# Four small moves in a fused MoBA and retention block: x reloaded from ScalarE's queue, more products at the first columns, two chunks put ahead of MoBA, the last broadcasts in other banks

## The chip, the cores and the metric

The kernel runs on one core of a Trainium2 chip. The core has five engines that run side by side: PE (TensorE, matrix products, with its weight loads shown apart as PEld), DVE (VectorE), ACT (ScalarE), POOL (GpSimd) and SP (SyncE, which here only starts transfers). PE writes its results to PSUM, which has eight banks of 128 x 512 floats. Everything else is kept in SBUF. The metric is the device time of one execution in microseconds (us). PE's clock stands at one of two levels, 1.2 or 2.4 GHz, and the profile gives what was granted as a share of the higher one.

## What is computed

One decoder block on 512 tokens of width 1024, all in float32. The core of the reference:

```
ada = silu(c) @ w_ada + b_ada            # 6 vectors: sh1, sc1, g1, sh2, sc2, g2
h = rms_norm(x, ln1_w) * (1 + sc1) + sh1
mq, mk, mv, rq, rk, rv, rg, ga, gr = split(h @ w_in)
a_out = moba_attention(rope(mq), rope(mk), mv)       # 8 heads of 64, blocks of 256
r_out = head_group_norm(retention(rope(rq), rope(rk), rv))   # 8 heads, values of 128
merged = sigmoid(ga) * (a_out @ w_moba_o) + sigmoid(gr) * ((silu(rg) * r_out) @ w_ret_o)
x = x + g1 * (merged @ w_out)
h2 = rms_norm(x, ln2_w) * (1 + sc2) + sh2
x = x + g2 * (square(relu(h2 @ w_ff1)) @ w_ff2)      # inner width 4096
return rms_norm(x, final_norm_w)
```

MoBA lets a query see its own block of 256 keys causally, and the chosen fully past blocks. With 512 tokens there are two blocks, so the choice is only whether the first is seen by the second. Retention is causal attention with a decay per head in place of the softmax, and each head's output is normalised by its own mean and variance.

## The kernel before

**Products.** Each float32 operand is split into a high part and a remainder (`hi`, `lo`). A product is three matmuls (`mm3`, lines 220 to 223): high by high, and the two mixed ones. For a weight tile of 128 x 1024, ACT makes `whi` (line 188) and POOL makes `wlo` in four pieces of 256 columns (line 182). The raw weights land in a ring of three buffers (`load_raw`, line 175), and the split ones have four buffers each. A raw buffer is free again when POOL has read it.

**First columns (lines 324 to 343).** The six adaLN vectors come from sums over `w_ada`. ACT and DVE add the products of each column block into `adaacc`, and PE turns the sums to columns (`ada_columns`, line 283). DVE forms the shift and scale `mod` (lines 288, 289), ACT applies them to the transposed x in bank PT and writes the high part `hh` (lines 302, 303), and DVE writes the remainder `hl` (line 306). PE's first real products (lines 373, 376) wait for `hh`. Until then the function `busy(n)` (line 133) issues n matmuls of ones by ones into a bank that nobody reads. `busy(3)` stands behind the first column sums.

**MoBA and the chunks.** While attention runs, PE also does the projections that are still owed. They stand in `queue` as generators, one for each 256 output columns. One step of such a generator is a chunk of two k-tiles, six matmuls. `fill(n)` issues the next n chunks. The first queue holds 11 generators of 8 chunks: 88. Ahead of MoBA `fill(9)` issues nine. Then come the scores of the first head in four tiles (`moba_scores`, lines 596, 597), with two chunks behind each, and one more chunk. In each of the 8 heads there are four turns. A turn transposes the probabilities into the one PT bank (`moba_turn`, line 627). ACT and DVE split them (`th`, `tl`, lines 227, 230), and PE multiplies the turn before with the values (`moba_values`, lines 635, 636). Two chunks may be issued after each turn and one more at each head's start. That is 9 + 8 + 1 + 72 = 90 places for 88 chunks. PE's order is written out by hand; the orders of ACT, DVE and POOL in this stretch are set by the scheduler. The rotations of later projections (`rope`: copies on ACT in line 511, DVE lines 515 to 523; `qs` in lines 534, 535; `kh`, `kl` in lines 551 to 556) stand in a list `later`, a few of whose steps are taken at each turn. The softmax of a tile is DVE lines 602 to 611, ACT's Exp in line 612 and ACT's scaling copy in line 614.

**Retention's norm.** `ret_norm(h)` (line 784) broadcasts a row of factors over the partitions by one matmul into bank PT, and DVE reads it (`zf`, line 786). For heads 4 to 7 it is called one after the other with two chunks behind each, while the owed gates `gr` are projected.

**Output projection and second norm.** `merge` forms `merged` k-tile by k-tile (DVE lines 1029 to 1033, ACT's `mh` in line 1032). PE multiplies it with `w_out`, the first half of the columns into `wo0`, then the second half with weights `woh`, `wol` (ACT line 227 and POOL line 230 of `load_late`). `x2` is x loaded again, 512 KB for each of four token tiles, issued on SP (line 1082). Its buffers lie where tiles of the merge lay. `residual` (lines 1096, 1097) multiplies a product by g1 and adds it to `x2`. `square` (lines 1108, 1109) takes the sum of squares and its root on ACT; the root needs another table in ACT than the one before. `scale2` (lines 1113, 1114) scales on DVE, `turn2` transposes on PE (line 1124), DVE and ACT apply the second shift and scale (lines 1131, 1129), and DVE splits to `h2h` and `h2l` (lines 229, 230 again). Then the MLP's first products start (`ff1_part`). Here the orders of PE, DVE and ACT are written by hand: the products of token tile t, its residual, its square, and behind the products of tile 2 the transposes of tile 0.

## Time and profile before

| | |
|---|---|
| time, median of 3 runs | 882.7 us (882.34 to 882.77) |
| the profiled execution's own time | 883.12 us |
| its span, first to last instruction | 881.3 us |
| mean granted clock | 0.991 |
| busy: PE / DVE / ACT / POOL | 847.6 / 458.6 / 407.1 / 500.1 us |
| moved by DMA | 108.41 MB, mean 123 GB/s |

The time of an execution has 1.8 us around the span. Times in the rows are counted from the span's start. In the list of instructions a row shows when it starts, how long it takes, the engine, the line and operation, what is written from what, and in brackets how long the engine had been idle before it and what ended that wait. A row with x2 merges two neighbours. PE's matmuls overlap: one of 512 columns shows 0.39 us, but the next starts 0.227 us later.

### The profile page before, as it was taken

The numbers are of one execution on the slowest core, as the hardware profiler recorded it, in microseconds if no ns is written. First come the engines' busy times: TensorE is split into PE (matmuls) and PEld (weight loads), VectorE is DVE, ScalarE is ACT, GpSimd is POOL, SyncE is SP. The second block draws the span as 40 slices with busy tenths as digits, with TensorE's granted clock in tenths as the row PEclk, the third lists the DMA queues.
The fourth block names the chain that finished last, engine by engine and source line by source line (L and its number), as shares of the span: only waits on it lengthen the run. The fifth ranks groups of instructions, "written<-read, shape, count | busy, mean of one in ns | idle before, by whom it ended". The sixth has DMA issues, their size and how long they took to land. (4 is left out here: it accounts for less than half of the span.)

```text
span 881.3 us, 11801 instructions
## 1 busy us (share of the span) xinstructions
PE 847.6 (96%) x4138; PEld 708.8 (80%) x4138; DVE 458.6 (52%) x897; ACT 407.1 (46%) x697; POOL 500.1 (57%) x622
## 2 busy tenths in 40 slices
PE   7899999999999999999999899999999999999996
PEld 4777877898788898788887689888888888888885
DVE  5877677677878879853466584203304022222224
ACT  4558988897645547654223243223332211222124
POOL 3465445346545456565546366977777755555564
PEclk9999999999999999999999989999999999999998
DMA  9964222313363443413453633533433232322302
GB/s 278 305 201 132 72 72 72 97 48 97 102 198 120 130 146 111 153 48 96 157 178 119 239 106 97 180 96 121 142 96 96 96 99 97 100 103 98 100 25 96
DMA packets 104426, 108.41 MB, mean 123 GB/s; under 512 B 4832, under 2 KB 93360, under 8 KB 104368
## 3 DMA queue, kind: packets, MB, share of 16 engines
q1 hardware_dynamic: 104224, 107.47, 39.4%
q8 instruction: 32, 0.52, 0.3%
q14 instruction: 26, 0.21, 0.1%
q10 hardware_dynamic: 144, 0.20, 0.1%
HBM read 105.55 MB, written 2.10 MB: 122 GB/s over the span
## 5 line engine op out<-in xcount | busy, mean ns | idle before, releaser
L182 POOL TENSOR_TENSOR wlo<-raw,whi 128x256 fp32r<-128x256 f32 x524 | 409.1, 813 | 284.6 <-ACT whi L188 243.1
L188 ACT ACTIVATE whi<-raw 128x1024 fp32r<-128x1024 f32 x126 | 132.7, 1058 | 189.8 <-PE ps_O L223 104.9
L221 PE MATMUL ps_acc<-hh,whi 128*128 128x512 f32 x304 | 119.8, 394 | 0.0
L222 PE MATMUL ps_acc<-hl,whi 128*128 128x512 f32 x304 | 118.7, 391 | 0.0
L223 PE MATMUL ps_acc<-hh,wlo 128*128 128x512 f32 x304 | 118.7, 390 | 0.0
L221 PE MATMUL ps_acc<-h2h,whi 128*128 128x512 f32 (+1 forms) x288 | 106.2, 369 | 1.1 <-DVE h2h L229 1.1
L222 PE MATMUL ps_acc<-h2l,whi 128*128 128x512 f32 (+1 forms) x288 | 106.2, 369 | 0.3 <-DVE h2l L230 0.3
L223 PE MATMUL ps_acc<-h2h,wlo 128*128 128x512 f32 (+1 forms) x288 | 106.0, 368 | 0.0
L229 DVE CAST fh<-act 128x512 fp32r<-128x512 f32 x32 | 16.2, 515 | 132.5 <-PE ps_O L222 132.5
L223 PEld LDWEIGHTS ps_acc<-hh,wlo 128*128 128x128 f32 x304 | 57.1, 188 | 12.4
L221 PEld LDWEIGHTS ps_acc<-hh,whi 128*128 128x128 f32 x304 | 57.2, 188 | 10.2
L222 PEld LDWEIGHTS ps_acc<-hl,whi 128*128 128x128 f32 x304 | 57.2, 188 | 10.1
L221 PEld LDWEIGHTS ps_acc<-h2h,whi 128*128 128x128 f32 x288 | 54.9, 190 | 10.1 <-DVE h2h L229 1.6
L222 PEld LDWEIGHTS ps_acc<-h2l,whi 128*128 128x128 f32 x288 | 54.9, 191 | 9.3 <-DVE h2l L230 0.7
L223 PEld LDWEIGHTS ps_acc<-h2h,wlo 128*128 128x128 f32 x288 | 55.0, 191 | 8.8
L222 PE MATMUL ps_acc<-wlo,fh 128*128 128x512 f32 (+1 forms) x136 | 52.1, 383 | 0.0
L223 PE MATMUL ps_acc<-whi,fl 128*128 128x512 f32 (+1 forms) x136 | 52.1, 383 | 0.0
L221 PE MATMUL ps_acc<-whi,fh 128*128 128x512 f32 (+1 forms) x136 | 52.1, 383 | 0.0
L847 DVE SCALAR_TENSOR_TENSOR ada_acc<-ada_raw,cact,ada_acc 128x256 f32<-128x256 f32 x48 | 31.2, 649 | 31.9 <-DMA ada_raw<-in_w_ada_dram 31.0
L1201 ACT ACTIVATE relu<-ps_acc 128x512 f32<-128x512 f32 x32 | 18.8, 588 | 62.4 <-PE ps_acc L223 62.4
L823 DVE TENSOR_TENSOR g<-g,ps_acc 128x256 f32<-128x256 f32 x4 | 1.7, 421 | 80.1 <-PE ps_acc L822 80.1
L1202 POOL TENSOR_TENSOR act<-relu 128x512 f32<-128x512 f32 x32 | 34.5, 1078 | 14.1 <-ACT relu L1201 14.0
(291 smaller groups left out, 1861.3 us busy)
## 6 DMA issues: line engine op xcount, KB each, us to landing
raw<-in_w_ff_dram SPq DMA_DIRECT2D x64, 512.0 KB, 3.5
raw<-in_w_in_dram SPq DMA_DIRECT2D x32, 512.0 KB, 3.7
ada_raw<-in_w_ada_dram SPq DMA_DIRECT2D x64, 256.0 KB, 3.1
raw<-in_w_in_dram SPq DMA_DIRECT2D x36, 256.0 KB, 3.5
wada<-in_w_ada_dram SPq DMA_DIRECT2D x32, 256.0 KB, 5.2
x<-in_x_dram SPq DMA_DIRECT2D x8, 512.0 KB, 6.0
raw<-in_w_ret_o_dram SPq DMA_DIRECT2D x8, 512.0 KB, 3.6
dec<-in_k_decay_dram SPq DMA_DIRECT2D x8, 256.0 KB, 4.6
```

Of the source, the lines that this page charges most:

```text
L182: eng.tensor_sub(lo[:, cs], src[:, cs], hi[:, cs].bitcast(F32))
L188: ACT.activation(hi, raw, AF.Copy)
L221: PE.matmul(o, lh, rh, start=first, stop=False)
L222: PE.matmul(o, lh, rl, start=False, stop=False)
L223: PE.matmul(o, ll, rh, start=False, stop=last)
L229: eh.tensor_copy(hi, src)
L823: DVE.tensor_add(dst[:, n0 : n0 + 256], dst[:, n0 : n0 + 256], cp[:, 0:256])
L847: eng.scalar_tensor_tensor(acc, raw[:, 0, :], cact[:, 2 * k2 : 2 * k2 + 1], acc, op0=ALU.mult, op1=ALU.add)
L1201: ACT.activation(r, a, AF.Relu)
L1202: POOL.tensor_mul(act[n], r, r)
```

## The change

Five edits, four of them moves:

- `busy(3)` behind the first column sums becomes `busy(7)`: four more matmuls of ones.
- `fill(9)` ahead of MoBA becomes `fill(11)`: two chunks move from the end of the queue's run to its start.
- `ret_norm` of heads 4 to 7 takes a bank of tag S (three banks) in place of PT (one).
- The four loads of `x2` go from SP's queue to ACT's, and are to stand behind ACT's last `mh` copy.
- A root of one column, whose result nobody reads, is put on ACT behind the same copy, so that ACT's table for roots is loaded there.

```
@@ first columns
     cp = ada_columns(a)
-    busy(3)
+    busy(7)
     mod = modulation(0, cp)
@@ ret_norm
-        rp = ps("PT")
+        rp = ps("PT" if h < 4 else "S")
@@ ahead of MoBA
-    fill(9)
+    fill(11)
     for t in (3, 2, 1, 0):
         moba_scores(0, t)
         fill(2)
@@ reload of x
     for t in range(NT):
         x2.append(B.tile([P, D], F32, name=f"x2_{t}"))
-        dma(x2[t], xs[t * P : (t + 1) * P, :])
+        with tc.issue_after(merged[-1]):
+            ACT.dma_start(x2[t], xs[t * P : (t + 1) * P, :])
@@ behind the definition of residual
+    root = W2.tile([P, P], F32, name="root")[:, :1]
+    with tc.issue_after(merged[-1]):
+        ACT.activation(root, epsc, AF.Sqrt)
     for t in range(NT):
         residual(W2, t, 0, wo0[t], g1)
```

ACT at the end of the merge, before. `mh` is the last of the merge, `woh` are weights of the second half, `y,rs` is the square of a token tile, `whi` a weight tile of the MLP:

```order
L1032 ACTIVATE mh_4636<-m_5110 128x512
L227 ACTIVATE woh_5281<-raw 128x512
L227 ACTIVATE woh_5287<-raw 128x512
L1108 ACTIVATE y_5308,rs_5309<-x_0_5235 128x1024
L1109 ACT_TABLE_LOAD
L1109 ACTIVATE rs_5309<-rs_5309,epsc 128x1
L188 ACTIVATE whi<-raw 128x1024 x2
```

The same place now:

```order
L1032 ACTIVATE mh_4640<-m_5114 128x512
L1084 DMA x_0_5239<-in_x_dram 128x1024
L1084 DMA x_1_5241<-in_x_dram 128x1024
L1084 DMA x_2_5243<-in_x_dram 128x1024
L1084 DMA x_3_5245<-in_x_dram 128x1024
L227 ACTIVATE woh_5287<-raw 128x512
L227 ACTIVATE woh_5293<-raw 128x512
L1104 ACT_TABLE_LOAD
L1104 ACTIVATE root<-epsc 128x1
L1114 ACTIVATE y_5314,rs_5315<-x_0_5239 128x1024
L1115 ACTIVATE rs_5315<-rs_5315,epsc 128x1
L188 ACTIVATE whi<-raw 128x1024 x2
```

Four loads stand ahead of the last two `woh` copies, the fourth of them with a wait for the transfer of the first of these two copies' raw weights, and the table load has left the place between the square and its root. On SP the four loads of x are gone from between the MLP's first raw tile and the loads of g2 and the final norm's weights.

ACT behind the `kh` copies of the first MoBA head, before, up to just ahead of the scaling copy of the last of the head's four tiles (128x128):

```order
L605 ACTIVATE pr,stat<-ps_S 128x256
L612 ACT_TABLE_LOAD
L612 ACTIVATE pr,stat<-ps_S,stat 128x512
L706 ACTIVATE gate_904<-ps_acc 128x512
L612 ACTIVATE pr,stat<-ps_S,stat 128x384
L614 ACTIVATE pr<-pr,stat 128x512
L614 ACTIVATE pr<-pr,stat 128x384
L612 ACTIVATE pr,stat<-ps_S,stat 128x256
L188 ACTIVATE whi<-raw 128x1024
L614 ACTIVATE pr<-pr,stat 128x256
L612 ACTIVATE pr,stat<-ps_S,stat 128x128
L706 ACTIVATE gate_960<-ps_acc 128x512
```

The same place now, up to the scaling of the third tile:

```order
L534 ACTIVATE qs<-roped 64x512
L511 ACTIVATE sw<-ps_acc 32x512 x2
L605 ACTIVATE pr,stat<-ps_S 128x256
L612 ACT_TABLE_LOAD
L612 ACTIVATE pr,stat<-ps_S,stat 128x512
L188 ACTIVATE whi<-raw 128x1024
L614 ACTIVATE pr<-pr,stat 128x512
L612 ACTIVATE pr,stat<-ps_S,stat 128x384
L612 ACTIVATE pr,stat<-ps_S,stat 128x256
L614 ACTIVATE pr<-pr,stat 128x384
L614 ACTIVATE pr<-pr,stat 128x256
```

Between the `kh` copies and the scaling copy of the last tile there now stand three copies of line 511, both copies of line 534 and one weight copy of line 188 more than before; the rest is the same work in another order.

PE at the last MoBA head, now. In the order before, the two turns stood with two chunks (twelve matmuls) between them:

```order
L627 MATMUL ps_PT<-ident,pr 128x128 x2
L635 MATMUL ps_O<-th,vm_724 128x384
L636 MATMUL ps_O<-tl,vm_724 128x384
L627 MATMUL ps_PT<-ident,pr 128x128
L635 MATMUL ps_O<-th,vm_751 128x256
L636 MATMUL ps_O<-tl,vm_751 128x256
L635 MATMUL ps_O<-th,vm_754 128x128
L636 MATMUL ps_O<-tl,vm_754 128x128
```

Nothing stands between the third turn's transposes (x2) and those of the fourth but the products of the turn before. From the first retention scores on PE's order is as before.

## Rows read from the trace of the kernel before

**Rows 1.** Page part 1, then stages: length, busy per engine, PEclk, DMA share, GB/s

```profile
PE 847.6 (96%) x4138; PEld 708.8 (80%) x4138; DVE 458.6 (52%) x897; ACT 407.1 (46%) x697; POOL 500.1 (57%) x622
...
95.00:225.00 130.00, 125.81 (x704) 106.95 (x703) 93.97 (x263) 109.61 (x237) 63.51 (x78) 1.00 0.25 75
...
507.00:518.00 11.00, 11.00 (x48) 8.76 (x45) 9.23 (x16) 4.52 (x10) 9.80 (x11) 0.84 0.34 97
518.00:526.00 8.00, 6.52 (x40) 6.15 (x40) 6.39 (x14) 5.18 (x13) 3.57 (x4) 0.79 0.23 66
```

**Rows 2.** Instructions in order of time, PE, end of the output projection

```profile
501.87 0.39 PE L223 MATMUL ps_acc<-woh,ml 128*128 128x512 f32 x1
506.25 1.09 PE L1124 MATMUL ps_S<-ident,y 128*128 128x128 f32 x8 [4.00 <-DVE y L1114]
...
519.15 0.38 PE L221 MATMUL ps_acc<-h2h,whi 128*128 128x256 f32 x1 [1.14 <-DVE h2h L229]
```

**Rows 3.** The same, DVE

```profile
492.12 1.28 DVE L1096 TENSOR_TENSOR u<-ps_S,g 128x512 f32<-128x512 f32 x2
496.47 0.69 DVE L1097 TENSOR_TENSOR x<-x,u 128x512 f32<-128x512 f32 x1 [3.06 <-DMA x<-in_x_dram]
497.74 0.69 DVE L1097 TENSOR_TENSOR x<-x,u 128x512 f32<-128x512 f32 x1 [0.58 <-DMA x<-in_x_dram]
...
518.66 0.43 DVE L229 CAST h2h<-h 128x512 fp32r<-128x512 f32 x1
```

**Rows 4.** The same, ACT: the last mh copy, and the table load

```profile
485.42 0.63 ACT L1032 ACTIVATE mh<-m 128x512 fp32r<-128x512 f32 x1 [1.32 <-DVE m L1031]
...
503.62 1.28 ACT L1109 ACT_TABLE_LOAD   x1
```

**Rows 5.** The same, SP's queue: a raw weight load, the first two loads of x

```profile
486.01 0.33 SPq L175 DMA_DIRECT2D raw<-in_w_out_dram  x1
...
489.38 0.97 SPq L1082 DMA_DIRECT2D x<-in_x_dram  x2
```

**Rows 6.** x's tile, issue to landing; then a stage of 1 us

```profile
DMA to landing us min/median/max: 7.0/7.4/7.7
...
485.00:486.00 1.00, 1.00 (x6) 0.82 (x5) 0.38 (x1) 0.58 (x1) 1.00 (x2) 1.00 0.00 0
```

**Rows 7.** In order of time, PE ahead of and in the first head's scores

```profile
77.50 0.49 PE L596 MATMUL ps_S<-kh,qs 128*128 128x512 f32 x1 [0.72 <-ACT kh L552]
78.75 0.50 PE L597 MATMUL ps_S<-kl,qs 128*128 128x512 f32 x1 [0.75 <-DVE kl L556]
```

**Rows 8.** In order of time, ACT, and PE at the first head's first turn

```profile
80.35 1.20 ACT L511 ACTIVATE sw<-ps_acc 32x512 f32<-32x512 f32 x2
...
90.65 0.42 ACT L614 ACTIVATE pr<-pr,stat 128x128 f32<-128x128 f32 x1
90.94 1.07 ACT L188 ACTIVATE whi<-raw 128x1024 fp32r<-128x1024 f32 x1
91.89 1.29 ACT L534 ACTIVATE qs<-roped 64x512 fp32r<-64x512 f32 x2
...
93.57 0.60 PE L627 MATMUL ps_PT<-ident,pr 128*128 128x128 f32 x4
```

**Rows 9.** In order of time, the last head: DVE, then PE

```profile
221.72 2.31 DVE L535 TENSOR_TENSOR qs<-roped,qs 64x512 fp32r<-64x512 f32 x2
...
224.31 0.33 PE L635 MATMUL ps_O<-th,vm 128*128 128x128 f32 x1 [0.74 <-ACT th L227]
```

**Rows 10.** In order of time, PE at the first columns; then a stage of 1 us

```profile
19.23 1.65 PE L373 MATMUL ps_acc<-whi,hh 128*128 128x512 f32 x3 [1.44 <-ACT hh L303]
...
23.87 0.61 PE L283 MATMUL ps_O<-ones,adaacc 128*128 128x2 f32 x4 [0.97 <-DVE adaacc L356]
...
20.00:21.00 1.00, 1.00 (x4) 0.80 (x3) 0.96 (x3) 0.74 (x1) 0.18 (x1) 0.50 1.16 289
```

**Rows 11.** In order of time, PE at a broadcast of ret_norm

```profile
413.93 0.40 PE L784 MATMUL ps_PT<-both,es 128*128 128x512 f32 x1
```

More of the change, by code (lines that the diff above doesn't have):

```diff
@@ L338, in block_kernel @@
     cp = ada_columns(a)
-    busy(3)
+    busy(7)
     mod = modulation(0, cp)
@@ L781, in ret_norm @@
     def ret_norm(h):
-        rp = ps("PT")
+        rp = ps("PT" if h < 4 else "S")
         PE.matmul(rp, es[:, h % 4 : h % 4 + 1].to_broadcast([P, P]), rstd_rows[h // 4], start=True, stop=True)
@@ L936, in block_kernel @@
     pinned.__enter__()
-    fill(9)
+    fill(11)
     for t in (3, 2, 1, 0):
@@ L1081, in block_kernel @@
         x2.append(B.tile([P, D], F32, name=f"x2_{t}"))
-        dma(x2[t], xs[t * P : (t + 1) * P, :])
+        with tc.issue_after(merged[-1]):
+            ACT.dma_start(x2[t], xs[t * P : (t + 1) * P, :])
     g2 = B.tile([P, D], F32, name="g2")
@@ L1097, in residual @@
         DVE.tensor_add(x2[t][:, hs], x2[t][:, hs], u)
+    root = W2.tile([P, P], F32, name="root")[:, :1]
+    with tc.issue_after(merged[-1]):
+        ACT.activation(root, epsc, AF.Sqrt)
     for t in range(NT):
```

## The prediction, made before the changed kernel was run

> **What bounds the kernel now.** I read the busy times first. PE is busy for 847.6 of 881.3 us [rows 1], so an edit pays only where PE idles or runs at the lower clock. The other engines matter only where PE waits for them. Next I read PE's instructions in order of time, for the waits in brackets. The longest by far is 4.00 us ahead of the transposes of token tile 0, for DVE's scaled tile; a second of 1.14 us stands ahead of the MLP's first product, for `h2h` [rows 2]. The other places that the change touches are small: 0.72 and 0.75 us at the first scores [rows 7], 1.44 and 0.97 us at the first columns [rows 10]. The stretch of MoBA idles PE for 130 less 125.81, so 4.2 us, in many small waits [rows 1]. Last come the rows of the engines that PE waits for.
>
> **The reload of x and the table load.** Before, DVE has its first two products `u` done at 492.12 + 1.28 = 493.40 and then stands for x, 3.06 us and again 0.58 us [rows 3]. SP issued x only at 489.38 [rows 5], because its queue was held at the raw weight loads ahead. Behind DVE's last addition ACT squares, then loads a table for 1.28 us [rows 4], then takes the root, and DVE scales. All of this is one chain, so the most that goes from it is 3.06 + 0.58 + 1.28 = 4.92 us.
>
> Does x come in time? ACT's queue reaches the loads when the last `mh` copy ends, at 485.42 + 0.63 = 486.05 [rows 4], 3.3 us sooner than SP did. The slowest x took 7.7 us to land [rows 6]: 493.75, against 493.40 where DVE asks. The earlier loads stood behind a raw tile of 512 KB; these start when the DMA engines carry nothing (0 GB/s from 485 to 486 [rows 6]). I take no wait; the bound is 0.35 us for the first. The fourth load waits until one raw weight tile, issued at 486.01 [rows 5], has landed. DVE asks for it five operations of at most 0.69 us later, near 496.7, so it must be issued by about 489. If the issue slips to 490, up to 1 us is lost.
>
> The Trainium skill has a rule that speaks against this edit: "DMA: Bandwidth & Descriptors", section "Issuing engines are not separate DMA queues", says that loads issued from ScalarE and SyncE run on the same 16 engines and interleave, so that a second issuing queue saves only the time to issue. By that rule alone the 3.64 us would stay and only the table load would pay. The idle engines at 485 to 486 us speak for the row: what was late was the start.
>
> Who pays on ACT? Two `woh` copies now stand behind the four loads. Two issues took 0.97 us on SP [rows 5], four on ACT therefore about 2 us, more if the fourth's wait is longer. PE reaches the transposes of tile 0 at 502.10 (below) behind 36 matmuls of tiles 1 and 2, 8.2 us, so it ends tile 0 at 493.9 and takes up these two weights from 492.5 on, 6.5 us after the loads begin, with POOL's remainder between. A slip of one or two us delays PE, and the following shows that PE has that much room. The new table load lies where ACT waits for DVE anyway.
>
> What is late next? The scaled tile comes at 506.25 − 4.92 = 501.33, and PE gets there at 501.87 + 0.23 = 502.10 [rows 2], so the 4.00 us vanish. Up to the MLP's first product PE then has the work that it did from 506.25 to 518.01, 11.76 us. In that stretch the granted clock was 0.84 of full over 11 us [rows 1], the lower of the two levels behind a wait of four us; at full clock 0.16 × 11 = 1.8 us of it go. PE would be there at 502.10 + 10.0 = 512.1. But `h2h` hangs on DVE's chain: 518.66 + 0.43 = 519.09 before [rows 3], 514.17 now. So PE waits 2.1 us there in place of 1.14, and what is won is DVE's 4.92 us, not PE's 4.00 + 1.8. The lower clock behind this point (0.79 over 8 us [rows 1]) I leave as it is, since a wait stays in front of it. Sum: **−4.9 us**, between −1.3 (x no sooner) and −7.0 (all of PE's wait gone, 519.15 − 512.1).
>
> **Two chunks in front of MoBA.** A chunk is six matmuls 0.227 us apart, 1.36 us; two are 2.7 us. PE was free at 77.50 − 0.72 = 76.78 and is now busy until 79.5, past the 78.75 at which `kl` let it go [rows 7]. Both waits go: **−1.5 us**.
>
> The chunks come from the end, and ACT's order behind them is another one. Ahead of the last scaling copy of the first head ACT now does three more copies of line 511 (half of 1.20 each), two of line 534 (1.29) and one weight copy (1.07) [rows 8]: 1.80 + 1.29 + 1.07 = 4.2 us. That copy ended at 90.65 + 0.42 = 91.07, and would end near 95.2. PE transposed at 93.57 [rows 8] and now gets there at 93.57 + 2.7 − 1.5 = 94.8. So 2.5 us of room become a wait of about 0.4. Idle that the profile counts between matmuls is some tenths short of the distance between their starts, so PE may be there sooner: I take **+0.7**, between 0 and +2.
>
> At the last head the two turns that lost their chunks follow each other. The fourth turn's transposes need bank PT, so they wait for `th` and `tl` of the third. Uncovered, that is one copy and one subtraction less two products, about 0.5 us. DVE now has two `qs` subtractions (2.31 us as a pair [rows 9]) ahead of that `tl`, so at most 2.8 us. I take **+1.5**. The 0.74 us at the last product [rows 9] stay. The rest of the 4.2 us of small waits is shuffled with the order, ±1.5 us. Sum of this edit: **+0.7 us**, between −1.5 and +4.
>
> **The other two.** `busy(7)` adds four matmuls, 0.9 us. PE is free at 19.23 − 1.44 = 17.79 [rows 10] and would be done at 18.70, still ahead of `hh`. Before, the granted clock fell behind that wait (0.50 from 20 to 21 us [rows 10]). Kept up, PE is through sooner and then waits longer at 23.87 for DVE's sums, which ask nothing of PE's clock. I take 0. The gain is at most a tenth or two at the column sums; the loss has its own case below. For `ret_norm` in S the broadcast shows no wait in front of it [rows 11], with chunks between two of them: 0.
>
> **The sum.** −4.9 + 0.7 = −4.2 us. The profiled execution took 883.1 us, so 878.9; the median of the three runs lies 0.4 us lower, which gives **878.5 us**.
>
> **The rivals.**
> - *The shift of chunks is free.* The new waits at the first and last head don't show; for it speaks that my 0.7 and 1.5 are each near the edge of what PE's arrival covers. −4.9 − 1.5 = −6.4, so 876.3 us.
> - *x comes no sooner.* The three loads and the raw weights share the engines, the fourth load holds ACT, and DVE still stands for 3.6 us; only the table load pays. For it speaks the load of that stretch, where x took 7 us; against it the empty engines at 485. −1.3 + 0.7, so 882.1 us.
> - *The low clock moves.* PE, through sooner with its first products, stands for over two us ahead of 23.87, and the clock falls behind that wait instead, where PE has eighteen products to do before it waits again. A low stretch costs 0.21 × 8 = 1.7 us [rows 1], so 880.2 us at worst. The Trainium skill's "TensorE: Matmul & The Clock Gate", section "HAM oscillation — how this bites in real kernels", describes just this, a burst between two long waits that starts at the lower clock each time. The 0.50 of the row agrees.
> - *ACT becomes the bound in MoBA: slower.* ACT is busy for 109.61 of 130 us there [rows 1], and every turn needs its `th`. With chunk copies two places ahead, each of the 28 turns of the seven further heads may find `th` late. At 0.4 us, about half of the 0.74 us that one such wait costs [rows 9], that is +11.2: 878.5 + 11.2 = 889.7 us. It makes the whole slower by over 0.2% from about 0.22 us a turn on. Against it: total ACT work is the same, and 20 us of ACT's time are free.
> - *An edit that does nothing*: the `ret_norm` one, as I expect, and `busy(7)` if the clock falls all the same. Neither moves the time.
>
> **How the numbers follow.** Forecast 0.50 (its own range 876.5 to 880.5), free shift 0.20, x no sooner 0.12, low clock 0.10, ACT bound 0.06, something else 0.02. The range reaches from a little below the free shift to just under x no sooner: 875.5 to 881.8; outside lie the slower case, half of x no sooner and the tails. A measurement here can tell 0.2%, 1.8 us, from no change. Faster than 880.9 us: most of the forecast, the free shift and most of the clock's case, 0.74. Within: x no sooner and the rests, 0.19. Slower: 0.07.
>
> **What would show it.** In the profile after: x's loads on ACT near 486 us, no DVE wait for x over 0.4 us, no table load between the first square and its root. PE without a wait at the transposes of tile 0, and one of about 2 us at the first `h2h` product, 4.9 us sooner against the merge's end. No PE wait at the first scores, a new one of under 2 us at the first turn, and one of 1 to 2 us between the third and fourth turn of the last head. I am wrong if DVE still stands for x, if PE's idle time in the MoBA stretch is above 8 us, or if the MLP's first product comes more than 6 us sooner.

## The result: slower by 0.6%

The changed kernel took 887.42 us, median of six runs (885.59 to 891.66), against 882.52 us for the kernel before beside it. The ratio is 1.0058, interval 1.0039 to 1.0077. I had forecast 878.5 (875.5 to 881.8): the sign is wrong, and the time lies outside the range. The profiled execution of the changed kernel took 885.92 us, its span is 884.1 us, 2.8 more than before.

First the page's part 1, then four stages of the changed kernel (length, busy time per engine, PEclk, DMA share, GB/s), against [rows 1]:

```profile
PE 847.3 (96%) x4142; PEld 708.9 (80%) x4142; DVE 461.7 (52%) x897; ACT 407.9 (46%) x698; POOL 498.4 (56%) x622
...
95.00:225.00 130.00, 122.63 (x692) 104.84 (x692) 90.85 (x258) 106.59 (x230) 60.42 (x75) 1.00 0.25 75
225.00:250.00 25.00, 22.16 (x98) 18.08 (x96) 19.66 (x31) 13.32 (x23) 14.14 (x17) 0.93 0.42 126
507.00:518.00 11.00, 10.26 (x54) 8.41 (x53) 7.52 (x15) 7.13 (x13) 7.44 (x9) 1.00 0.17 52
518.00:526.00 8.00, 4.86 (x26) 3.64 (x24) 7.79 (x15) 3.78 (x8) 3.52 (x5) 1.00 0.45 132
```

PE's total is the same; what changed is where it idles. In the MoBA stretch its idle time went from 130 less 125.81, so 4.2 us, to 7.4 us.

PE's instructions in order of time, the changed kernel, with the idle time and its cause in brackets:

```profile
19.30 0.96 PE L373 MATMUL ps_acc<-whi,hh 128*128 128x512 f32 x3 [0.23 <-ACT hh L303]
23.59 0.61 PE L283 MATMUL ps_O<-ones,adaacc 128*128 128x2 f32 x4 [2.20 <-DVE adaacc L356]
...
79.30 0.39 PE L596 MATMUL ps_S<-kh,qs 128*128 128x512 f32 x1
...
95.05 0.66 PE L627 MATMUL ps_PT<-ident,pr 128*128 128x128 f32 x4 [0.31 <-ACT pr L614]
...
100.31 0.52 PE L627 MATMUL ps_PT<-ident,pr 128*128 128x128 f32 x3 [1.40 <-DVE tl L230]
...
158.12 0.33 PE L596 MATMUL ps_S<-kh,qs 128*128 128x128 f32 x1 [2.60 <-ACT pr L612]
...
227.96 0.33 PE L627 MATMUL ps_PT<-ident,pr 128*128 128x128 f32 x1 [2.37 <-DVE tl L230]
...
228.72 0.33 PE L635 MATMUL ps_O<-th,vm 128*128 128x128 f32 x1 [0.19 <-ACT th L227]
...
499.25 0.50 PE L222 MATMUL ps_acc<-wol,mh 128*128 128x512 f32 x1 [0.84 <-POOL wol L230]
...
510.57 1.09 PE L1130 MATMUL ps_S<-ident,y 128*128 128x128 f32 x8 [0.74 <-DVE y L1120]
...
523.44 0.39 PE L221 MATMUL ps_acc<-h2h,whi 128*128 128x256 f32 x1 [2.67 <-DVE h2h L229]
```

Read against the rows of before, three stretches tell the story.

- **First scores and first turn.** The waits of 0.72 and 0.75 us [rows 7] are gone. The first turn comes at 95.05 in place of 93.57 [rows 8], with two chunks (2.7 us) more done by then and only 0.31 us of new wait: PE is 1.2 us ahead.
- **The heads.** The last product of the stretch comes at 228.72 in place of 224.31 [rows 9], 4.4 us late. With the 1.2 us that PE was ahead, 5.6 us were lost between the first turn and there; PE waits 0.28 us more right behind it, at 229.33.
- **The reload.** The MLP's first product comes at 523.44 in place of 519.15 [rows 2], 4.3 us late, so almost nothing was won on the way. The 4.00 us ahead of the transposes of tile 0 [rows 2] became 0.74, but PE now stands for `wol` (0.84 us, and 0.73 a little later) and 2.67 us ahead of `h2h`. From ACT's last `mh` copy to that product it was 519.15 − 485.42 = 33.73 us [rows 2, 4]; now, with that copy at 490.71, it is 32.73.

Behind that product 1.5 us come back in this execution, about what the clock there is worth: from 518 to 526 the granted clock is 1.00 where it was 0.79 [rows 1], and 0.21 × 8 is 1.7 us. That makes 4.3 − 1.5 = 2.8 us of span.

What PE waited for from 95 to 235 us (engine, line waited for: us in total, times, longest), the kernel before:

```profile
PE ps_PT L627 <- DVE tl L230: 1.4, 3, 0.7
...
PE ps_S L596 <- ACT pr L612: 0.6, 1, 0.6
```

The same of the changed kernel:

```profile
PE ps_PT L627 <- DVE tl L230: 4.7, 4, 2.4
PE ps_S L596 <- ACT pr L612: 4.0, 2, 2.6
```

These two causes alone are 6.7 us more. Six waits make them up, and four of the six, of 1.40, 2.60, 1.42 and 2.37 us, make up 7.8 of the 8.7 us.

### The profile page after: what moved, and what is told of

Read it like the earlier page. It is cut to its first block, busy times and chain, and to the rows that moved or that the text cites. A ratio compares the mean times of both kernels' runs of the same rounds, so it can differ in the third digit from the quotient of the medians.

```text
span 884.1 us, 11812 instructions
## 1 busy us (share of the span) xinstructions
PE 847.3 (96%) x4142; PEld 708.9 (80%) x4142; DVE 461.7 (52%) x897; ACT 407.9 (46%) x698; POOL 498.4 (56%) x622
## 5 line engine op out<-in xcount | busy, mean ns | idle before, releaser
L222 PEld LDWEIGHTS ps_acc<-hl,whi 128*128 128x128 f32 x304 | 57.5, 189 | 10.2
```

The source lines that it names most:

```text
L222: PE.matmul(o, lh, rl, start=False, stop=False)
```

## Experiments

Each run's time is compared with runs of the kernel before on the same chip. Unless the table says otherwise, a run is the kernel before with that edit alone. An interval that holds 1 means that the run can't be told from the kernel before.

| run | edit | ratio to before | interval |
|---|---|---|---|
| e1_fill11 | the two chunks alone | 1.0070 | 1.0046 to 1.0094 |
| e2_fill9 | the whole change but the chunks | 0.9985 | 0.9971 to 1.0000 |
| e3_xroot | x on ACT's queue, early root | 0.9984 | 0.9970 to 0.9997 |
| e4_root | early root | 0.9995 | 0.9981 to 1.0009 |
| e5_fill10 | one chunk | 1.0054 | 1.0036 to 1.0073 |
| e6_skip | two chunks, last head covered again | 1.0014 | 0.9997 to 1.0031 |
| e7_xlane | e3, no hold on ACT | 0.9994 | 0.9976 to 1.0013 |
| e8_xsplit | two loads of x on ACT, two on SP, root | 0.9976 | 0.9962 to 0.9990 |
| e9_front | two chunks, taken from the first scores | 1.0021 | 1.0006 to 1.0036 |
| e10_prio11 | e1, other priorities | 1.0071 | 1.0052 to 1.0090 |
| e11_prio9 | before, other priorities | 1.0003 | 0.9988 to 1.0017 |
| e12_late | root, g2 later | 0.9985 | 0.9971 to 0.9999 |
| e13_behind11 | e1, rotations behind the splits | 1.0026 | 1.0013 to 1.0038 |
| e14_exp11 | e13, and behind Exp | 1.0088 | 1.0070 to 1.0106 |
| e15_behind9 | before, rotations behind the splits | 0.9979 | 0.9965 to 0.9993 |
| e16_both | e8 and e15 | 0.9940 | 0.9922 to 0.9957 |
| e17_all9 | e16, busy(7), ret_norm in S | 0.9933 | 0.9914 to 0.9952 |
| e18_busy7 | busy(7) alone | 0.9990 | 0.9974 to 1.0005 |

### Which edit loses

```
# e1_fill11
-    fill(9)
+    fill(11)
```

> The kernel before with fill(11) in place of fill(9) and nothing else. Theory (the shift of two chunks is what costs): the last product of MoBA comes 4 to 5 us later, as it did in the changed kernel, nothing behind it wins, so 882.5 + 4.4 = 887 us (885 to 889). Rival one (what I forecast: the shift costs 0.7, and the loss comes from the other edits): 883 us. Rival two (the shift costs only together with the low clock that busy(7) moved): 882 to 884, with PE idle under 6 us from 95 to 225.

```
# e2_fill9: the changed kernel, with
-    fill(11)
+    fill(9)
```

> The changed kernel with fill(9) back; the other four edits stay. Theory (only the shift costs; the reload wins the table load and about 1 us of the wait for x, up to 2 us more where PE's clock does not fall ahead of the MLP): 879.5 to 882, about 881. Rival (one of the other four edits costs 4 us): 885 to 887. If the reload did what I forecast: 878.

Measured: 889.36 us for the chunks alone and 881.63 for the rest, beside 883.23 for before. The two chunks cost 6.1 us and the other four edits win 1.6, which is at the edge of what can be told from none; together 4.5, about the change's 4.9. In the two traces ACT and DVE run the same instructions in the same order through MoBA, and the waits in the heads of e1_fill11 are those of the changed kernel to 0.2 us: 1.38, 0.60, 2.60, 0.68, 1.24 and 2.38 us. The other four edits don't take part in it.

```
# e3_xroot
-        dma(x2[t], xs[t * P : (t + 1) * P, :])
+        with tc.issue_after(merged[-1]):
+            ACT.dma_start(x2[t], xs[t * P : (t + 1) * P, :])
...
+    with tc.issue_after(merged[-1]):
+        ACT.activation(root, epsc, AF.Sqrt)
```

> The kernel before with x on ScalarE's queue and the early root, without the other three edits. Theory (the fourth load of x holds ScalarE for about 6 us, so the wait for x goes from the first tile to the fourth): about 1 us sooner at the MLP's first product, 881.5 us. Forecast of the prediction: 4.9 us sooner, 877.6. Rival (busy(7) and the banks of ret_norm are worth nothing): this equals the run with fill(9) back to 0.5 us; if busy(7) costs or wins, the two differ by that.

```
# e4_root: the last two lines of that alone
```

> The kernel before with only the early root: the table load leaves the chain from DVE's additions to the MLP's first product, x stays on SyncE. Theory (the chain of DVE and ACT sets that product): 1.28 us sooner, 881.2 us, with the waits for x still 3.06 and 0.58. If so and the run with x on ScalarE's queue as well is no faster, x's move is worth nothing or costs. Rival (the chain is not what sets it): 882.5.

Measured: 881.82 and 882.14 us beside 883.23. From the last `mh` copy to the MLP's first product, 33.73 us before, it is 31.73 with the root alone (x waits of 1.87, 0.58 and 0.52 us there) and 31.04 with x on ACT's queue as well. The waits for x in e4_root come to 2.97 us, 0.67 less than the 3.64 before, and with the table load's 1.28 that makes 1.95 of the 2.0 us. So in the trace the table load pays as worked out; in e4_root's time (0.9995) it can't be told from none. Moving x adds 0.7 us in e3_xroot's trace, and none in e2_fill9's (31.80). By the times alone the three can't be told apart. e3_xroot and e2_fill9 are equal, as expected of `busy(7)` and `ret_norm`.

### Why the reload wins so little

The changed kernel's trace, ACT and its queue at the reload, then DVE, then what the view of x's tile gives from issue to landing:

```profile
490.71 0.63 ACT L1032 ACTIVATE mh<-m 128x512 fp32r<-128x512 f32 x1 [1.66 <-DVE m L1031]
490.71 6.45 ACTq L1084 DMA_DIRECT2D x<-in_x_dram  x4
497.22 0.64 ACT L227 ACTIVATE woh<-raw 128x512 fp32r<-128x512 f32 x1 [5.88 <-DMA raw<-in_w_out_dram]
...
499.21 1.28 ACT L1104 ACT_TABLE_LOAD   x1
...
497.42 1.28 DVE L1098 TENSOR_TENSOR u<-ps_S,g 128x512 f32<-128x512 f32 x2
498.62 2.81 DVE L1099 TENSOR_TENSOR x<-x,u 128x512 f32<-128x512 f32 x2
...
505.87 0.69 DVE L1099 TENSOR_TENSOR x<-x,u 128x512 f32<-128x512 f32 x1 [2.64 <-DMA x<-in_x_dram]
...
497.93 2.95 POOL L230 TENSOR_TENSOR wol<-raw,woh 128x512 fp32r<-128x512 f32 x2 [3.72 <-ACT woh L227]
...
DMA to landing us min/median/max: 3.7/6.3/8.9
```

The first x is there in time (3.7 us), and DVE does not stand for it any more. But the four issues take 6.45 us, because the fourth waits for the landing of the raw `woh` tile, as I had seen. What I had not seen: three loads of x, issued from 490.71 on, run ahead of that raw tile or beside it on the same engines and make it late. The tile is issued at 491.30 and lands 5.5 us later, where it was 2.9 before. ACT waits 5.88 us for it, where it waited 2.85 before. So the fourth x is issued at 496.83, and DVE stands 2.64 us for it.

The late tile costs a second time. POOL makes `wol` later, and its subtractions now run beside DVE's first two additions, which take 1.13 and 1.76 us in place of 0.69 each (2.81 us as a pair). So the two waits of 3.64 us went, and 2.64 us of another wait and 1.4 us of slower additions came. Counted from the last `mh` copy, the first square starts 17.34 us later, where it was 17.04: x's move lost 0.3 us. The table load's 1.28 us then make it the 1.0 us that were won.

```
# e7_xlane: e3_xroot, and
-    dma(g2, b_ada[0:1, 5 * D : 6 * D].to_broadcast([P, D]))
-    dma(fw, final_norm_w.rearrange("(o n) -> o n", o=1).to_broadcast([P, D]))
...
             load_ff1(t)
+            if t == 2:
+                with tc.issue_after(last_raw[0]):
+                    dma(g2, b_ada[0:1, 5 * D : 6 * D].to_broadcast([P, D]))
+                    dma(fw, final_norm_w.rearrange("(o n) -> o n", o=1).to_broadcast([P, D]))
```

With the loads of g2 and fw moved, none of the four loads of x was to have a wait.

> The kernel before with x on ScalarE's queue and the early root, and the loads of g2 and of the final norm's weights issued two raw weight tiles later. The four loads of x then lie on transfer semaphores that are long free, so the fourth has no wait. Theory (what held the fourth load ate the gain): no hold on ScalarE's queue, no wait of VectorE for x over 0.4 us, the copies of woh sooner by up to 3 us; but the raw woh tiles share the engines with four loads, and the waits of TensorE for wol (0.5 to 1.6 us with x on ScalarE) stay or grow. The MLP's first product then stands 3 to 4.5 us sooner than before against the last mh copy; 879.5 us. Rival (bandwidth: the loads and the raw tiles take what they take): wol later by another 1 to 2 us, TensorE waits there, no sooner than with the root alone; 881.5 to 882.5.

e7_xlane, ACT and its queue, then DVE's additions for tiles 2 and 3, then PE, then the last two raw `w_out` tiles, one by one, in the list of transfers (KB, us to landing):

```profile
486.76 1.84 ACTq L1086 DMA_DIRECT2D x<-in_x_dram  x4
...
496.66 0.63 ACT L229 ACTIVATE woh<-raw 128x512 fp32r<-128x512 f32 x1 [3.20 <-DMA raw<-in_w_out_dram]
...
497.09 2.35 DVE L1099 TENSOR_TENSOR x<-x,u 128x512 f32<-128x512 f32 x2
...
497.34 0.50 PE L223 MATMUL ps_acc<-woh,mh 128*128 128x512 f32 x1 [1.74 <-ACT woh L229]
498.94 0.80 PE L224 MATMUL ps_acc<-wol,mh 128*128 128x512 f32 x1 [1.10 <-POOL wol L232]
...
raw<-in_w_out_dram SPq DMA_DIRECT2D x1, 256.0 KB, 5.5
raw<-in_w_out_dram SPq DMA_DIRECT2D x1, 256.0 KB, 8.1
```

The same list in e4_root, where x is issued behind the raw tiles (three tiles, the median):

```profile
raw<-in_w_out_dram SPq DMA_DIRECT2D x3, 256.0 KB, 3.0
```

The hold is gone (four issues in 1.84 us), and so is every wait of DVE for x. The raw tiles pay: 5.5 and 8.1 us in place of 3.0, and PE stands 3.4 us for `woh` and `wol`: the two waits shown and 0.57 us at 494.87. The time is that of before (0.9994), and 33.74 us lie between the `mh` copy and the first product, as before. The rival of that run was right, and not my theory: here the bytes took their time, and what was issued first chose who waited. The Trainium skill says in "DMA: Bandwidth & Descriptors", section "Issuing engines are not separate DMA queues", that transfers started by different engines run on the same 16 DMA engines and interleave; the raw tiles that SP issued, late behind ACT's loads, agree (5.5 and 8.1 us in place of 3.0).

```
# e8_xsplit: e7_xlane, but
+        if t < 2:
+            with tc.issue_after(merged[-1]):
+                ACT.dma_start(x2[t], xs[t * P : (t + 1) * P, :])
+        else:
+            dma(x2[t], xs[t * P : (t + 1) * P, :])
```

> The kernel before with the early root, the loads of x for tiles 0 and 1 on ScalarE's queue, those for tiles 2 and 3 left on SyncE behind the MLP's first raw tile, and the loads of g2 and of the final norm's weights two raw tiles later. With all four loads on ScalarE and free of waits, VectorE no longer waited for x, but the raw woh tiles landed 5.4 to 6.8 us after issue in place of 3, and TensorE waited 3.4 us for woh and wol. Theory (the sixteen engines' bandwidth is what x and the raw tiles share, and the order of the bytes decides): with two loads ahead in place of four the raw woh tiles land about 2 us sooner, the waits of TensorE for woh and wol fall to 0.5 to 1.5 us, VectorE waits under 1 us for the tiles 2 and 3; the MLP's first product 3 to 4 us sooner than before against the first woh product, 879 to 880.5. Rival (any x ahead of the raw tiles costs TensorE what it saves VectorE): 881.5 to 882.5, the same as with the root alone.

```
# e12_late: e4_root, with g2 and fw later as in e7_xlane
```

> The kernel before with the early root and the loads of g2 and of the final norm's weights two raw tiles later; x stays on SyncE. It tells what of the run with split loads of x comes from the later g2. Theory (g2 was issued behind x and takes little from it): the same as with the root alone, 881.5 to 882.2, VectorE's first wait for x 1.9 to 3 us. Rival (1 MB fewer on the engines makes x land 1 to 2 us sooner): 880 to 881.

e8_xsplit: the raw tiles, DVE's only wait for x, and the MLP's first product:

```profile
raw<-in_w_out_dram SPq DMA_DIRECT2D x4, 256.0 KB, 5.0
...
501.96 0.69 DVE L1102 TENSOR_TENSOR x<-x,u 128x512 f32<-128x512 f32 x1 [0.62 <-DMA x<-in_x_dram]
...
519.87 0.38 PE L223 MATMUL ps_acc<-h2h,whi 128*128 128x256 f32 x1 [2.53 <-DVE h2h L231]
```

Measured 880.49 us for the split and 881.27 for e12_late, beside 882.88. With only the two loads ahead that DVE needs first, the last two raw tiles land 5.3 and 4.6 us after issue, PE has no wait for `woh` or `wol`, and 30.65 us lie between the `mh` copy and the first product, 3.1 less than before. The root with the later g2, without that split, leaves 32.41. So in the traces the order of the bytes wins what four loads ahead did not; the times of the two runs, 0.8 us apart, can't be told apart. Whether the two loads need ACT's queue, or only an earlier place on SP's, was not tried.

### Why two chunks cost so much

Changed kernel, ACT and DVE ahead of the wait of 1.40 us at 100.31. The transposes of the turn ran at 95.05:

```profile
97.53 0.63 ACT L551 ACTIVATE kh<-roped 64x512 fp32r<-64x512 f32 x1 [1.30 <-DVE roped L523]
98.19 0.63 ACT L552 ACTIVATE kh<-roped 64x512 fp32r<-64x512 f32 x1
98.84 0.60 ACT L227 ACTIVATE th<-ps_PT 128x512 fp32r<-128x512 f32 x1
...
96.38 1.11 DVE L523 TENSOR_TENSOR roped<-roped,sw 128x512 f32<-128x512 f32 x1
...
99.47 0.69 DVE L230 TENSOR_TENSOR tl<-ps_PT,th 128x512 fp32r<-128x512 f32 x1 [0.38 <-ACT th L227]
```

ACT idles for 1.30 us with a `kh` copy at the head of its queue whose sum `roped` isn't there yet, while `th`, which could have run, stands behind two such copies. With two chunks more at the front, the projections end two places sooner, and the steps of their rotations meet other turns.

The two longest waits are of another kind: there rotation steps that do run stand in front. Ahead of the 2.60 us at 158.12 (DVE, then ACT), and ahead of the 2.37 us at 227.96 (DVE):

```profile
155.18 0.69 DVE L519 TENSOR_TENSOR sw<-sw,rope 128x512 f32<-128x512 f32 x1
156.45 0.68 DVE L523 TENSOR_TENSOR roped<-roped,sw 128x512 f32<-128x512 f32 x1
157.29 0.69 ACT L612 ACTIVATE pr<-ps_S,stat 128x512 f32<-128x512 f32 x1 [1.16 <-DVE stat L607]
...
225.17 2.28 DVE L535 TENSOR_TENSOR qs<-roped,qs 64x512 fp32r<-64x512 f32 x2 [0.70 <-ACT qs L534]
227.48 0.42 DVE L230 TENSOR_TENSOR tl<-ps_PT,th 128x256 fp32r<-128x256 f32 x1
```

At 158.12 PE needs the bank that Exp of the 128x512 tile frees. These two rotation steps, and one of line 515 at 153.23, stand on DVE between the steps of that tile's softmax; in the kernel before none of the three does, and Exp started 8.6 us after the tile's scores where it is 9.6 now. At 227.96 PE needs `tl`, which stands behind two `qs` subtractions; its `th` is there only 0.3 us before they end, behind two `qs` copies and a weight copy on ACT.

Two theories stood against each other: this order on ACT and DVE makes the waits, or PE has too little cover at the places that lost their chunk.

```
# e5_fill10
-    fill(9)
+    fill(10)
```

> The kernel before with fill(10): one chunk moved to the front of MoBA in place of two. Theory one (the loss is the cover that the chunks took with them, at the last head and inside): about half of fill(11)'s, 1.5 to 3 us, so 884.5 to 886, with a wait of 1.0 to 1.6 us at the last head. Theory two (every shift gives ScalarE and VectorE another order, and the waits inside the eight heads come of that order): the waits at the last head shrink as said, but those inside stand at other turns than with nine or eleven chunks and add up to anything from 2 to 7 us; 882 to 888. My forecast of before: 882.8.

```
# e6_skip: fill(11), and
-            if kt == 0:
+            if kt == 0 and h not in (3, 5):
                 fill(1)
```

> The kernel before with fill(11), and the extra chunk at the start of heads 3 and 5 left out, so that the last head has its chunks again as before. Theory (the last head's missing cover costs about 2 us, the order of ScalarE and VectorE in the heads about 4): the 2.4 us at the last head become 0.7, the waits of 1.4 and 0.6 us in the first two heads stay; 1.5 to 2.5 us under fill(11), 885 to 888. Rival one (the missing cover at the end was all of it): 881.7, the gain at the first scores kept. Rival two (a head without its extra chunk waits at its first turn instead): equal to fill(11), with new waits of 1 us each at the first turns of heads 3 and 5.

```
# e9_front: fill(11), and
         moba_scores(0, t)
-        fill(2)
+        fill(2 if t > 1 else 1)
```

> The kernel before with fill(11) and one chunk in place of two behind the last two of the first head's four score tiles: two chunks move by a few us inside the first head's scores, and every place from the first turn on holds the chunk it held before. Theory (the loss of fill(11) comes from the heads): none of the waits of 1.2 to 2.6 us inside the heads and at the last head, the 0.72 and 0.75 us at the first scores gone, up to 1.5 us given back at the first turn; 881 to 883. Rival (any other order of ScalarE at the first head carries on through the heads): new waits of over 1 us inside the heads, 884 or more.

Measured: 887.82 (one chunk), 884.92 (last head covered again) and 885.22 us (first scores), beside 882.78. One chunk costs nearly what two do, and its waits are other ones: 2.02 us at the last head's first turn, 1.69 and 1.43 us elsewhere inside, beside 1.53 us at the last head's fourth turn, as both theories had it. So the loss doesn't go by the number of chunks. In e6_skip the last head's wait is back at 0.74 us, but 1.36 and 1.60 us stay inside. The 2.60 us are gone there too, and the time can't be told from that of the kernel before: better than my theory had it. But ACT's and DVE's orders differ as well from head 3 on, so this run doesn't say whether the cover or the order did it. In e9_front every place from the first turn on is as before, and so is every wait of over 0.4 us in the later heads (0.74, 0.41, 0.51, 0.60, 0.74); only the first head got new ones, 1.31 us for the bank that Exp frees and 0.94 us at its first turn. By its time this run went with its rival and not with my 881 to 883: the first head alone lost 0.21%.

```
# e10_prio11: fill(11); e11_prio9: fill(9); in both
+        with tc.high_priority(offset=40):      # softmax of a tile
...
-        with tc.high_priority(offset=20):      # split of a turn
+        with tc.high_priority(offset=60):
```

> The kernel with fill(11) alone, and in the scheduler's order on ScalarE and VectorE the softmax of a tile and the split of a turn go ahead of the rotations of later heads. TensorE's order is that of fill(11), matmul for matmul; only the order of ScalarE and VectorE in the heads is another one. Theory (the waits inside the heads are made by rotations that stand ahead of a tile's softmax or a turn's split): the 1.4, 0.6, 2.6, 0.7 and 1.2 us inside the heads shrink to the 2.5 us in all that the kernel before has, or less, the 2.4 at the last head to 1; 882 to 885. Rival (the chunks' places on TensorE make them: with two chunks fewer the same work of ScalarE and VectorE has too little cover): within 1 us of fill(11), 887 to 890.

> The kernel before, fill(9), with the same change of ScalarE's and VectorE's order as in the run before. Theory (order of those two engines, not TensorE's, sets the small waits inside the heads): a change of 1 us or more in either direction with TensorE's order untouched; if the rotations come too late instead, the next pair's scores wait for kh or kl. 880 to 886. Rival (order does not matter as long as TensorE's places are the same): 882.5, all waits within 0.2 us of those before.

Measured: 888.52 and 883.30 us beside 882.88, no gain in either. In e10_prio11 the first wait is 1.39 us again, with the same `kh` copies ahead of `th`; why the priority left them there, no run shows. In e11_prio9 the waits for `tl` did move (1.25 and 0.89 us are the longest, where it was 0.74), the time did not. So this pair didn't tell the theories apart. The next ones forced the order.

```
# e13_behind11: fill(11), every step of a rotation in
+            with tc.issue_after(behind[0]), tc.issue_after(behind[1]):   # th and tl of the turn ahead
+                step()
```

> fill(11) alone, TensorE's order unchanged, and on ScalarE and VectorE every step of a rotation is held behind the th and tl of the turn that stands ahead of it in the program. In the trace of fill(11) ScalarE waits 1.30 us for a rotation's sum ahead of the kh copies, and th of the first turn, whose transposes are long done, stands behind them. Theory (a step that is not ready at the head of an in-order queue holds the split behind it): the wait of 1.4 us at the second turn of the first head goes, that of 2.4 us at the last head falls under 1 us, the 2.6 and 1.2 us behind a tile's Exp may stay; PE idle in brackets from 75 to 235 under 7 us in place of 10; 883.5 to 886. Rival (TensorE's places alone make the waits): 888 to 889, idle of 9 us or more, as when only the priorities were changed.

```
# e14_exp11: the same, behind[0] also set by the tile's Exp, behind[1] by its scaled maximum
# e15_behind9: e13_behind11 with fill(9)
```

> The run before, and the rotations are held behind the last tile's Exp as well. Theory: the waits of 2.6 and 1.2 us for the bank that Exp frees go too; if the rotations come too late by that, the next pair's scores wait for kh and kl instead. 882.5 to 887. Rival: as in the run before, 888 to 889, the waits for Exp unchanged.

> The kernel before, fill(9), with the rotations held behind the turn's th and tl. Theory (order counts where a step at the head of the queue is not ready; with nine chunks the rotations already came behind the splits): the 0.74 and 0.43 us for tl go at best, 0 to 1.2 us less, 881.5 to 883. Rival (holding the rotations makes the next pair's kh late): waits at the first scores of a pair, 884 or more.

e13_behind11 at the place shown above: `th` of the first turn on ACT, and PE's transposes that had waited 1.40 us. Then what PE waited for from 95 to 235 us:

```profile
96.24 0.60 ACT L229 ACTIVATE th<-ps_PT 128x512 fp32r<-128x512 f32 x1 [0.39 <-PE ps_PT L637]
...
99.27 0.49 PE L637 MATMUL ps_PT<-ident,pr 128*128 128x128 f32 x3
...
PE ps_PT L637 <- DVE tl L232: 2.8, 4, 1.1
PE ps_S L606 <- ACT pr L622: 1.6, 2, 1.1
```

Measured: 885.65, 891.17 and 881.01 us beside 883.05. PE's 4138 matmuls run in e1_fill11's order. With that untouched, the order on ACT and DVE alone takes the loss of fill(11) from 0.70% to 0.26%; the two causes that make up 4.7 + 4.0 us in the changed kernel are 4.4 us here. Forcing too much (behind Exp as well) costs 0.9%, outside theory and rival: waits for `tl` of 6.5 us. With fill(9) the same order wins 2 us, and the waits for `tl` inside the heads fall from 1.4 us to 0.4. So the theory holds for the larger part of the loss, and not for all of it. At the last head a wait of 1.1 us is left in e13_behind11 where the chunks are missing, with two more of 0.45 and 1.21 us at its last products; and PE's idle time from 75 to 235 us fell from 10.2 to 8.2 us, not under the 7 that I had expected. Whether the 0.26% that remain are missing cover or an order still not good was not tried apart.

### Together, and busy(7)

```
# e16_both: e8_xsplit and e15_behind9
# e17_all9: e16_both with busy(7), and ret_norm of heads 4 to 7 in S
# e18_busy7: the kernel before with busy(7)
```

> The two edits that won by themselves together: the rotations behind the splits with fill(9), and the early root with x loaded half from ScalarE, half from SyncE, and g2 and the final norm's weights later. They lie 260 us apart on TensorE. Theory (they add): 2.0 + 2.4 us less than before, 878.5 us, 878 to 880. Rival (one eats the other, through the lower clock behind a shorter wait ahead of the MLP): 880 to 881.

> The run before with busy(7) and the last broadcasts of ret_norm in the scores' banks. Theory (both are worth nothing): the same within 0.5 us. Rival (four more products keep the clock up at the first columns): 0.5 to 1.5 us less. Rival (the longer wait behind them drops the clock later): 0.5 to 1.5 us more.

> The kernel before with busy(7) alone. Theory: 882.5 within 0.5 us; the granted clock is full from 20 to 21 us, where it was 0.50, and TensorE waits about 2.2 us ahead of the second column sums in place of 1.0. Rival (the low stretch moves behind that wait and is longer): up to 1.5 us more, the clock under 1 from 25 to 50 us.

e16_both, the MoBA stretch and the MLP's first product:

```profile
95.00:225.00 130.00, 127.50 (x715) 109.19 (x714) 94.35 (x265) 112.40 (x240) 67.42 (x80) 1.00 0.26 78
...
514.53 0.39 PE L223 MATMUL ps_acc<-h2h,whi 128*128 128x256 f32 x1 [1.51 <-DVE h2h L233]
```

Measured: 878.34, 877.13 and 882.62 us beside 883.73. The two gains, 0.24% and 0.21% by themselves, come together to 0.60% (0.43 to 0.78), so they add: PE's idle time in MoBA falls from 4.2 to 2.5 us, and 29.61 us lie between the last `mh` copy (484.92) and the first product, 4.1 less than before. e17_all9 is as fast within what can be measured. `busy(7)` alone is no change that can be told from none. In its trace (the first two lines) the clock is full where it was 0.50 [rows 10], and lower behind the next wait, from 25 to 50 us. But so it is in e4_root with `busy(3)` (the last two lines):

```profile
20.00:21.00 1.00, 1.00 (x6) 0.74 (x6) 0.96 (x3) 1.00 (x2) 0.00 (x0) 1.00 1.17 291
25.00:50.00 25.00, 24.30 (x111) 19.99 (x112) 21.42 (x48) 12.76 (x23) 9.98 (x12) 0.88 0.99 272
...
20.00:21.00 1.00, 1.00 (x6) 0.77 (x5) 0.96 (x4) 0.65 (x2) 0.00 (x0) 1.00 1.16 293
25.00:50.00 25.00, 24.33 (x117) 19.98 (x116) 22.48 (x49) 14.77 (x27) 10.13 (x12) 0.93 1.06 286
```

Of the sixteen traces with `busy(3)`, eleven show the full clock from 20 to 21 us and eleven a lower one (0.86 to 0.95) from 25 to 50; the four with `busy(7)` show 1.00 in the first place and 0.88 to 1.00 in the second. So the low stretch lies in one place or the other with either kernel, and its move can't be put down to the four products.

## Why the prediction was wrong, step by step

- **What bounds the kernel, and where PE waits:** right. Most of what was won or lost lies in the stretches named; the loss inside the heads was put at nothing there.
- **First scores, −1.5; first turn, +0.7:** right. Both waits went, and the first turn waits 0.31 us.
- **Last head, +1.5 (up to 2.8):** the right mechanism, the two `qs` subtractions ahead of `tl`, and about the size. 2.37 + 0.19 us stand where 0.74 was: 1.8 us, and 0.28 more right behind that product.
- **"The rest of the 4.2 us of small waits is shuffled with the order, ±1.5 us":** this step failed. Of the 5.6 us lost behind the first turn, 1.8 are the last head's; 3.8 are this term. I had taken it to come out at nothing on the average. But an order on ACT and DVE is made of single collisions. One cost 1.40 us, where a copy that wasn't ready held `th`, and one 2.60 us, where rotation steps stood on DVE between the steps of a softmax. The orders were there to be read row by row before the run: I read them at the first and the last head only.
- **The clock behind the long wait:** not in the sum. Behind the 2.37 us at the last head the granted clock from 225 to 250 us is 0.93, in e1_fill11 0.86, and 1.00 before. At 0.07 of 25 us that is 1.8 us in the changed kernel; 0.94 us of it is given back by a wait for `tl` at 231.12 in the trace of before that is gone. The kept traces agree: the six whose longest wait in the last head's later turns is 1.2 to 2.5 us show 0.86 to 0.93 from 225 to 250; the other fourteen, with 0.74 us there, show 1.00. It fits e1_fill11's median loss of 6.1 us, above the 4.4 at the last product here, but it was not tried apart.
- **The table load, −1.28:** right in the traces: it left the chain here, and e4_root's 2.0 us are this and 0.67 us of shorter waits for x.
- **The lower clock behind the MLP's first product, left as it is:** not so in this execution. It was 1.00 from 518 to 526 us where it was 0.79, and the 1.5 us of span that came back there stood in no term.
- **x's waits, −3.64:** this step failed; +0.3 was measured. The first x came in time as worked out, 3.7 us after issue. The bound for the fourth ("it must be issued by about 489") took the landing of the raw tile from the trace of before, 2.9 us. The loads in front of it made that 5.5, so the fourth load was issued 6.1 us behind the first and DVE stood 2.64 us for it; 1.4 us more went into additions that ran beside the late `wol`. The rival "x comes no sooner" was right in kind, and about in time: without the chunks, e2_fill9 and e3_xroot took 881.63 and 881.82 us, its figure was 882.1 with 0.7 for the chunks.
- **PE's room for a later `woh`:** too wide by 1.6 us, the two waits for `wol`.
- **ret_norm, 0, and busy(7), 0:** right as far as can be measured: e18_busy7 and the step from e16_both to e17_all9 can't be told from none. That the clock's low stretch hangs on `busy` is not borne out (above).
- **The rivals:** "ACT becomes the bound in MoBA" had the side and nearly the time (889.7), but its mechanism, 28 turns each late by 0.4 us, is not what happened: a handful of waits make the loss, 6.7 us more from two causes. The chance of 0.06 for it was too low, since the change reordered two engines through eight heads of which I had read two places. That the time came near is luck.

The sum of what was measured: −1.5 + 0.3 + 1.8 + 3.8 = +4.4 us at MoBA's last product; the 3.8 is what the other terms leave of it. From there to the last `mh` copy it is 262.0 us, where it was 485.42 − 224.31 = 261.1, so +0.9, with the low clock in it. Then +0.3 − 1.3 = −1.0 at the reload: +4.3 at the MLP's first product, and −1.5 behind it in this execution. Of my own signs of being wrong, one came true as written (DVE still stands for x); the idle time in MoBA stopped at 7.4 us, under the 8 that I had set, since the longest part of the last head lies behind 225 us.

## What to carry to other kernels

Where chunks of other work cover a latency, moving two of them moves every step that hangs on them on the other engines; price such an edit by reading the new order at each place, for a step that isn't ready, or a long one, ahead of one that PE waits for, and not by an average wait. Here holding such steps back by an explicit edge paid where a priority did nothing. Here a load that was issued sooner was paid by the transfers that it then stood in front of: ask which bytes are needed first, and put only those ahead.

## What the hardware showed that was not expected

- The last two raw tiles of 256 KB landed 2.9 and 3.1 us after issue where x came behind them (the kernel before), in 5.3 and 4.6 with two loads of x (512 KB each) issued first (e8_xsplit), in 5.5 and 6.0 with three (the changed kernel), and in 5.5 and 8.1 with four (e7_xlane).
- While x was landing and POOL made `wol`, one DVE addition of 128x512 took 1.76 us, where the same takes 0.69. Of the two, it is POOL that goes with it. In the kept traces 89 of these additions ran with no POOL instruction alongside and took 0.67 to 0.70 us, also with x landing (496.47 in [rows 3]). All 50 that took over 0.75 us ran beside a POOL subtraction; 21 more ran beside POOL work and took 0.71 us or less. Whether a transfer adds to it is open.
- In e7_xlane four issues from ACT took 1.84 us, so 0.46 each. In the changed kernel they took 6.45, since the fourth waits for a transfer, and ACT ran nothing from 491.34 to 497.22. What that hold alone costs the work behind it isn't shown: the copy that stood there needed the same raw tile.
